# Feed-forward blocks of a decoder trunk: the third block's matmuls on two 64-row tiles of the TensorE array

## Chip, cores, metric

One Trainium2 chip, one core. The metric is the device time of one execution in microseconds (us), as the median of several runs; lower is better. Engines are named as in the profile: PE is TensorE (matmuls), PEld its weight loads, DVE VectorE, ACT ScalarE, POOL GpSimd, SP SyncE, which issues most DMAs.

## What is computed

Two layers of a decoder, 256 tokens, width 1024. Each layer is a feed-forward stage, a token mixer and a second feed-forward stage, each followed by a layer norm:

```python
def _swiglu(x, w1, w3, w2):
    return (jax.nn.silu(x @ w1) * (x @ w3)) @ w2

for l in range(DEPTH):                                   # DEPTH = 2
    h = _swiglu(x, ffn_w1[l, 0], ffn_w3[l, 0], ffn_w2[l, 0])
    x = _layernorm(ALPHA * x + 0.5 * h, ln_g[l, 0], ln_b[l, 0])
    h = _mixer(x, l, ...)                                # gated spatial mixing and differential attention
    x = _layernorm(ALPHA * x + h, ln_g[l, 1], ln_b[l, 1])
    h = _swiglu(x, ffn_w1[l, 1], ffn_w3[l, 1], ffn_w2[l, 1])
    x = _layernorm(ALPHA * x + 0.5 * h, ln_g[l, 2], ln_b[l, 2])
```

x is 256 x 1024; w1 and w3 are 1024 x 2816, w2 is 2816 x 1024, all fp32. There are four feed-forward stages in all.

## The kernel before

**Products.** Each matrix product is made of three fp32r matmuls: an operand is split into a high part (`hi`, ScalarE rounds it to fp32r) and a low part (`lo`, VectorE subtracts), and hi x hi, lo x hi and hi x lo are added up in one bank of the matmul memory (PSUM). `three` (L253) issues them, L256 is the matmul. The contraction runs over the 128 rows of the array. The moving operand is 512 columns wide, one bank.

**Feed-forward stage (`ffn`, L599).** The 2816 inner columns are computed in five blocks of 512 (`for n in range(NB)`, L633) and two further groups (`gemm_a2`, L640), then multiplied by w2 (`gemm_b`). A block is one call of `gemm_b2` (L317); the very first block of the kernel is `gemm_first`. `gemm_b2` takes four banks: two token halves t of 128 tokens, times two matrices m (w1 and w3). The order of TensorE is written by hand: for t, for two halves c of the contraction, for m, for four k-tiles of 128 each: `rows_b` (L287) issues three matmuls per k-tile. So one block has 2 x 2 x 8 x 3 = 96 matmuls of 128 rows by 512 columns. Weights are loaded and split while t = 0 runs (`stream`, L152: a DMA of 1 MB by SyncE, then per 512 columns one ScalarE copy, L178, and one VectorE subtraction, L180) and used again for t = 1. There are eight buffers for each of the high and the low parts, so the next block's weights are split while t = 1 runs, as the buffers come free.

**The way out of a block (`front`, L605).** When a token half is done, `done` (L607) reads the two banks: ScalarE takes SiLU of the first (L612), VectorE multiplies by the second (L613). The result is transposed by POOL copies and a DMA (`transposed`, L204) and split into the operand of w2 (`turned`, L619; L629 and L631). These later steps are started by a counter of matmul work (`beat`).

**Who sets the order.** TensorE's order is that of the program. The other engines' instructions are ordered by a scheduler by priorities; `behind(...)` (L148) adds single constraints, such as that `done` for t = 0 is not placed ahead of the stage's last activation and subtraction of the norm (`latest`).

**Banks.** There are eight: four tagged "main" (`bank`, L78) and four tagged "side" (`side_bank`, L81), each group handed out in turn. In the feed-forward stages the blocks use main banks; side banks serve the mixer's attention and the norms' transposes.

**Two other places that the prediction reads.** The attention scores (`scores`, L698, matmul in L704) have a contraction of 64: plain fp32 matmuls of 64 rows, alternately from the upper and the lower 64 partitions, into two side banks. Each appears in the trace as two matmuls. The last norm (L508) has plain fp32 matmuls on all 128 rows.

Of the kernel before, what the change touches and what calls it, by code (L numbers as in the profile page):

```python
# [16 lines left out]
AF = mybir.ActivationFunctionType  # L17
# [3 lines left out]
P = 128  # L21
D = 1024
T = 256
NT = T // P
# [30 lines left out]
def trunk(ctx, tc, x, xT, w13a, w13b, w2, wb, wqk, wu, wg, wgr, wbr, wbrr, wo, gateb, gatebr, sgug, sgub, sguwT, sgubias, lam, diffg,  # L55
# [22 lines left out]
    def bank():  # L78
        return psum.tile([P, 512], F32, tag="main", name=name("bank"))
# [207 lines left out]
    def rows_b(ps, t, k0, piece, xh, xl, kts, c0=0, n=512, first=0):  # L287
# [6 lines left out]
                  k == first, k == (first - 1) % kts)  # L294
        beat(n / 1024)

    def gemm_b(src, kts, xh, xl, done, tail=4, last=()):

        blocks = [[(bank(), c, n) for c, n in (last if t else ()) or ((0, 512),)] for t in range(NT)]
        held = []  # L300
        for c in range(0, kts, 4):
            nk = min(4, kts - c)
            for i, piece in enumerate(stream(src[:, c * 512 : (c + nk) * 512], nk * 512)):
                k = c + 2 * i
                if k >= kts - tail:
                    held.append((k, piece))
                    continue
                for t in range(NT):
                    for ps, o, n in blocks[t]:
                        rows_b(ps, t, k, piece, xh, xl, kts, o, n)  # L310
        for t in range(NT):
            for ps, o, n in blocks[t]:
                for k, piece in held:
                    rows_b(ps, t, k, piece, xh, xl, kts, o, n)
                done(t, ps[:, :n], o, n)

    def gemm_b2(srcs, xh, xl, done, norm=None, second=(0, 1), each=None):  # L317

        lent, after = [()] * 4, [(None, None)] * 4
        if norm:
            lent = [(0, 1), (0,), (), ()]
            after[1:3] = (None, None if norm.front == 1 else norm.ends[0]), [norm.ends[0]] * 2
        ps = [[bank() for _ in range(2)] for _ in range(NT)]
        got = [[None] * 4 for _ in range(2)]
        for t in range(NT):
            order = second if t else (0, 1)
            for c in order:
                if norm:  # L330
                    norm.ready(t, c)
                    after[3] = [norm.ends[1]] * 2
                for m in range(2):
                    n = 2 * c + m
                    if t == 0:
                        got[m][2 * c : 2 * c + 2] = stream(srcs[m][:, c * CH : (c + 1) * CH], sub=512, lent=lent[n],
                                                           after=after[n], pool=(1,) if norm and norm.front == 1 and n == 1 else ())
                    for i in range(2 * c, 2 * c + 2):
                        rows_b(ps[t][m], t, 2 * i, got[m][i], xh, xl, KT, first=order[0] * KT // 2)
                    if each and c == order[1]:  # L340
                        each(t, m, ps[t][m])
            with behind(latest[0] if t == 0 else None):
                done(t, ps[t])

    def gemm_first(srcs, done):

        step()
        ps = [[bank() for _ in range(2)] for _ in range(NT)]
        raw = [[raw_pool.tile([P, CH], F32, tag="raw", name=name("raw")) for _ in range(2)] for _ in range(2)]
        for k0, nk in ((0, 1), (1, 1), (2, 1), (3, 1), (4, 2), (6, 2)):  # L350
            xr = slots("xraw", 2)[0][:, : nk * T]
            nc.sync.dma_start(xr, xT[:, k0 * T : (k0 + nk) * T])
            c, k = k0 // 4, k0 % 4
            if nk == 2 or k % 2 == 0:
                w = [[p.tile([P, HC], F32R, tag=n, name=name("w" + n)) for p, n in ((hi_pool, "hi"), (lo_pool, "lo"))]
                     for _ in range(2)]
            for m in range(2):
                (A if k0 + m == 0 else nc.sync).dma_start(raw[c][m][:, k * 512 : (k + nk) * 512],
                                                          srcs[m][:, k0 * 512 : (k0 + nk) * 512])
            x = x_cat[c][:, k : k + nk]  # L360
            split(x[:, :, :T], x[:, :, T:], xr.rearrange("p (k t) -> p k t", k=nk))
            ws = [[[v[:, (k + j) % 2 * 512 : (k + j) % 2 * 512 + 512] for v in w[m]] for m in range(2)]
                  for j in range(nk)]
            for j in range(nk):
                for m in range(2):
                    split(*ws[j][m], raw[c][m][:, (k + j) * 512 : (k + j + 1) * 512])
            end = k0 + nk == KT
            for ts in ((0,), (1,)) if end else ((0, 1),):
                for j in range(nk):
                    for m in range(2):  # L370
                        hi, lo = ws[j][m]
                        for y, o in ((hi, 0), (hi, T), (lo, 0)):
                            for t in ts:
                                PE.matmul(ps[t][m], x[:, j, o + t * P : o + (t + 1) * P], y,  # L374
                                          start=k0 + j == 0 and o == 0 and y is hi,
                                          stop=k0 + j == KT - 1 and y is lo)
                        beat(0.25 * len(ts))
                if end:
                    done(ts[0], ps[ts[0]])
# [219 lines left out]
    def ffn(l, f, i, norm, last=False):  # L599
        xh, xl = parts(both)  # L600
        h_hi = [act.tile([P, 512], F32R, tag="slot", name=name("hhi")) for _ in range(FT // 2)]
        h_lo = [act.tile([P, 512], F32R, tag="slot", name=name("hlo")) for _ in range(FT // 2)]
        hh, hl = view(h_hi), view(h_lo)

        def front(n, wait):  # L605

            def done(t, ps):  # L607
                pool, tag = ((act, "val"), (res, "bc"))[n % 2]
                p = pool.tile([P, D], F32, tag=tag, name=name("planes"), bufs=2).rearrange("p (w c) -> p w c", w=2)
                s = p[:, 1]  # L610
                with behind(norm.xhi[1, 0] if norm and (n, t) == (0, 0) else None):
                    silu[0] = A.activation(s, ps[0], AF.Silu).ins  # L612
                added[0] = V.tensor_tensor(out=s, in0=s, in1=ps[1], op=ALU.mult).ins  # L613
                beside(turned(n, t, s, p, wait[t]), 0)
                if norm is None and (n, t) == (1, 0):
                    beside(setup(s[:, :1]), 0)
            return done

        def turned(n, t, s, p, wait):  # L619
            lead = 3.5 if n == 0 and norm else 0  # L620
            yield from transposed(s, p[:, 0], p[:, 1], lead, wait - lead, 0.6, G)
            x = p[:, 0].rearrange("p (k t) -> p k t", k=4)
            yield 0.6
            for j in range(2):
                k = (n * 4 if n < NB - 1 else FT - 4) // 2 + j
                hi, lo = (v[k].rearrange("p (k t) -> p k t", k=2)[:, :, t * P : (t + 1) * P] for v in (h_hi, h_lo))
                f = x[:, 2 * j : 2 * j + 2]
                with behind(silu[0]):
                    A.activation(hi, f, AF.Copy)  # L629
                with behind(added[0]):  # L630
                    V.tensor_tensor(out=lo, in0=f, in1=hi.bitcast(F32), op=ALU.subtract)  # L631

        for n in range(NB):  # L633
            srcs = [w13b[l, f, m * NB + n] for m in range(2)]
            if n == 0 and norm is None:
                gemm_first(srcs, front(n, (10.3, 10.3)))
            else:
                gemm_b2(srcs, xh, xl, front(n, (13.3, 10.3)), norm=norm if n == 0 else None)
        for j in range(FA, FT - 4, 2):
            for m, z in gemm_a2([w13a[l, f, j - FA + m] for m in range(2)], both, lambda m: t512("silu")):  # L640
                s = z[:, :T]
                silu[0] = A.activation(s, s, AF.Silu).ins
                V.tensor_tensor(out=s, in0=s, in1=z[:, T:], op=ALU.mult)
                split(hh(j + m), hl(j + m), s)
        ln = Norm(l, i, 2.0 * ALPHA, 4.0 * EPS, s[:, :1], last)
        gemm_b(w2[l, f, 0], FT, hh, hl, lambda t, p, c, n: ln.part(t, 0, p))

        def done(t, p, c, n):
            ln.part(t, 512 + c, p)
            if c + n == 512:  # L650
                ln.finish(t, 1.9)

        gemm_b(w2[l, f, 1], FT, hh, hl, done, tail=14, last=((0, 256), (256, 256)) if last else ())
        return ln.close()

# [389 lines left out]
```

## Time and profile before

| | |
|---|---|
| median of 3 runs | 1209.79 us (1209.71 to 1209.86) |
| span of the profiled execution | 1208.3 us |
| what lies around the span, by the median | 1.5 us |
| TensorE busy | 1202.6 us, 5891 matmuls |
| VectorE busy | 903.2 us |
| ScalarE busy | 719.9 us |
| POOL busy | 332.9 us |
| fp32r matmuls of L256, 128 x 512, mean of one as recorded | 390 ns |

No time of the profiled execution other than its span is recorded, so the 1.5 us are the difference of the median and the span. A line of the trace names the source line, the engine, the operation, the tile written and the tiles read, the shape (partitions x elements), and the count. "64\*128" in a matmul's line is the part of the array that it uses, rows x columns. A matmul's recorded duration (390 ns) includes its way through the array, and successive matmuls overlap; how fast they follow each other is read from their starts. In the timeline the first number is the start in us from the beginning of the span, the second the time that the merged instructions took, and in brackets stands how long the engine had been idle before and what ended that. "L256" and the like are lines of the kernel before.

### The profile page before, as it was taken

What the parts mean: (1) busy time and instruction counts of PE and PEld (TensorE: products, weight loads), DVE (VectorE), ACT (ScalarE), POOL (GpSimd) and SP (SyncE); (2) the same over time, 40 slices, a digit from 0 to 9 for tenths busy, and PEclk for the clock granted to TensorE, in tenths of its full rate; (3) what the DMA queues carried; (4) which work ended last, traced back from release to release, by engine and by line L of the source; (5) the groups of instructions that cost most, each with busy time, mean ns of one, the idle gap of its engine ahead of it and who ended that gap; (6) DMA issues with size and microseconds to landing.
All of it is one profiled execution on the core that took longest, in us unless ns stands there. A gap on an engine that the chain in (4) does not pass through costs nothing.

```text
span 1208.3 us, 16816 instructions
## 1 busy us (share of the span) xinstructions
PE 1202.6 (100%) x5891; PEld 1013.3 (84%) x5891; DVE 903.2 (75%) x1544; ACT 719.9 (60%) x1388; POOL 332.9 (28%) x442
## 2 busy tenths in 40 slices
PE   9999999999999999999999999999999999999998
PEld 8888888888888888888888888888888888888887
DVE  6686669897689886766686756688966989776763
ACT  6465547668855665554555554576788556564740
POOL 1433101256421234330053330004464012423300
PEclk9999999999999999999999999999999999999999
DMA  9967646768765666767476766476676764877540
GB/s 347 303 219 238 253 174 203 259 200 231 240 213 180 200 231 208 249 201 261 149 245 198 259 187 261 148 273 238 211 205 199 251 192 153 274 231 239 186 181 35
DMA packets 124006, 263.58 MB, mean 218 GB/s; under 512 B 88417, under 2 KB 89489, under 8 KB 97809
## 3 DMA queue, kind: packets, MB, share of 16 engines
q1 hardware_dynamic: 119664, 248.80, 62.0%
q0 software_dynamic: 3824, 13.18, 3.4%
q8 instruction: 46, 0.75, 0.3%
q10 hardware_dynamic: 432, 0.52, 0.1%
q14 instruction: 40, 0.32, 0.1%
HBM read 236.52 MB, written 1.05 MB: 197 GB/s over the span
## 4 chain that ended last, share of the span: by engine, by line
PE 99%; DMA 0%; DVE 0%; ACT 0%; issue 0%; ACTq 0%
PE bank L256 72%; PE bank L268 15%; PE bank L275 8%; PE bank L374 2%; PE sbank L704 1%; PE sbank L760 1%; PE sbank L878 1%; DMA xraw<-in_xT 0%; PE sbank L758 0%; PE sbank L533 0%; PE sbank L512 0%; DVE xtok L520 0%; ACT whi L220 0%; DVE st L471 0%; DVE xtok L467 0%; ACT x L220 0%
## 5 line engine op out<-in xcount | busy, mean ns | idle before, releaser
L180 DVE TENSOR_TENSOR wlo<-raw,whi 128x512 fp32r<-128x512 f32 (+1 forms) x566 | 524.6, 962 | 114.8 <-ACT whi L178 80.0
L178 ACT ACTIVATE whi<-raw 128x512 fp32r<-128x512 f32 (+1 forms) x570 | 433.3, 799 | 246.6 <-PE bank L256 183.0
L256 PE MATMUL bank<-whi,x 128*128 128x512 f32 x1480 | 460.7, 390 | 0.0
L256 PEld LDWEIGHTS bank<-whi,x 128*128 128x128 f32 x1480 | 277.9, 188 | 57.7
L256 PE MATMUL bank<-wlo,x 128*128 128x512 f32 x740 | 288.0, 389 | 0.0
L256 PEld LDWEIGHTS bank<-wlo,x 128*128 128x128 f32 x740 | 139.0, 188 | 28.2
L268 PE MATMUL bank<-x,whi 128*128 128x512 f32 x640 | 153.3, 391 | 0.0
L256 PE MATMUL bank<-whi,hhi 128*128 128x512 f32 (+1 forms) x374 | 141.2, 378 | 0.0
L256 PE MATMUL bank<-wlo,hhi 128*128 128x512 f32 (+1 forms) x374 | 141.0, 377 | 0.0
L256 PE MATMUL bank<-whi,hlo 128*128 128x512 f32 (+1 forms) x374 | 140.9, 377 | 0.0
L193 POOL COPY planes<-planes 128x512 uint16<-128x512 uint16 x80 | 87.1, 1116 | 193.9 <-DVE planes L613 193.9
L268 PEld LDWEIGHTS bank<-x,whi 128*128 128x128 f32 x640 | 118.2, 188 | 23.8
L202 POOL COPY planes<-planes 128x512 uint16<-128x512 uint16 x80 | 70.9, 931 | 95.8 <-DMA planes<-planes 95.5
L613 DVE TENSOR_TENSOR planes<-planes,bank 128x512 f32<-128x512 f32 x40 | 27.4, 684 | 83.8 <-issue 69.3
L612 ACT ACTIVATE planes<-bank 128x512 f32<-128x512 f32 x40 | 23.9, 598 | 102.6 <-PE bank L256 101.5
L275 PEld LDWEIGHTS bank<-x,wlo 128*128 128x128 f32 x640 | 81.4, 191 | 2.9
L275 PE MATMUL bank<-x,wlo 128*128 128x256 f32 x640 | 82.6, 283 | 0.0
L256 PEld LDWEIGHTS bank<-whi,hlo 128*128 128x128 f32 x374 | 70.4, 188 | 13.0
L256 PEld LDWEIGHTS bank<-whi,hhi 128*128 128x128 f32 x374 | 70.4, 188 | 12.8
L256 PEld LDWEIGHTS bank<-wlo,hhi 128*128 128x128 f32 x374 | 70.4, 188 | 12.6
L575 POOL COPY nvia<-ntwo 128x256 uint16<-128x256 uint16 x20 | 10.4, 565 | 198.1 <-DMA ntwo<-nvia 179.9
L680 POOL TENSOR_TENSOR swap<-swap,sin_t 128x512 f32<-128x512 f32 x16 | 27.1, 1695 | 100.0 <-DMA swap<-z 78.0
(209 smaller groups left out, 1392.0 us busy)
## 6 DMA issues: line engine op xcount, KB each, us to landing
raw<-in_w13b SPq DMA_DIRECT2D x76, 1024.0 KB, 5.8
raw<-in_w SPq DMA_DIRECT2D x40, 1024.0 KB, 6.2
raw<-in_wb SPq DMA_DIRECT2D x16, 1024.0 KB, 5.1
raw<-in_wqk SPq DMA_DIRECT2D x16, 1024.0 KB, 6.3
raw<-in_w13a SPq DMA_DIRECT2D x8, 1024.0 KB, 5.1
raw<-in_wgr SPq DMA_DIRECT2D x8, 1024.0 KB, 5.3
raw<-in_wg SPq DMA_DIRECT2D x8, 1024.0 KB, 5.0
raw<-in_wu SPq DMA_DIRECT2D x8, 1024.0 KB, 6.4
```

Source lines behind the costliest of these rows:

```text
L178: A.activation(h, r, AF.Copy)
L180: eng.tensor_tensor(out=w, in0=r, in1=h.bitcast(F32), op=ALU.subtract)
L193: G.tensor_copy(out=planes(out)[:, w], in_=numbers(src)[:, w])
L202: eng.tensor_copy(out=numbers(out)[:, w], in_=planes(src)[:, w])
L256: PE.matmul(ps, xx, w, start=start and n == 0, stop=stop and n == 2)
L268: PE.matmul(b[-1], hi[:, k * P : (k + 1) * P], xc(k), start=k == 0, stop=False)
L275: PE.matmul(b[n][:, :T], lo[:, k * P : (k + 1) * P], xc(k)[:, :T], start=False, stop=k == KT - 1)
L374: PE.matmul(ps[t][m], x[:, j, o + t * P : o + (t + 1) * P], y, start=k0 + j == 0 and o == 0 and y is hi, stop=k0 + j == KT - 1 and y is lo)
L612: silu[0] = A.activation(s, ps[0], AF.Silu).ins
L613: added[0] = V.tensor_tensor(out=s, in0=s, in1=ps[1], op=ALU.mult).ins
L680: turned_by[0] = G.tensor_tensor(out=s3, in0=s3, in1=s, op=ALU.mult).ins
L704: PE.matmul(banks[m][:, j * nk : (j + 1) * nk], rows(qT, m, j, t * P, P), rows(kT, m, j, 0, nk), start=True, stop=True)
```

## The change

In every feed-forward stage, the third block (n = 2) is no longer done by `gemm_b2` but by a new `gemm_two`. Each 128-row matmul becomes two of 64 rows: the upper and the lower half of the contraction, on two 64-row tiles of the array in turn, each adding up in a bank of its own. A token half so needs four banks instead of two: t = 0 takes the four side banks, t = 1 the four main banks. On the way out ScalarE copies the second bank of each pair to SBUF and VectorE adds the first to it; SiLU and the product then read the sums from SBUF. The fourth block (n = 3) takes side banks for its first token half.

```diff
+    def rows_two(banks, t, k0, piece, xh, xl):
+
+        hi, lo = piece
+        for j in range(2):
+            k, s = k0 + j, slice(j * 512, (j + 1) * 512)
+            for n, (y, x) in enumerate(((hi, xh), (lo, xh), (hi, xl))):
+                for half in range(2):
+                    r = slice(half * P // 2, (half + 1) * P // 2)
+                    PE.matmul(banks[half], x(k)[r, t * P : (t + 1) * P], y[r, s], start=k == 0 and n == 0,
+                              stop=k == KT - 1 and n == 2)
+        beat(0.5)
+
+    def gemm_two(srcs, xh, xl, done):
...
+        got = [[None] * 4 for _ in range(2)]
+        for t in range(NT):
+            ps = [[(bank if t else side_bank)() for _ in range(2)] for _ in range(2)]
+            for c in range(2):
+                for m in range(2):
+                    if t == 0:
+                        got[m][2 * c : 2 * c + 2] = stream(srcs[m][:, c * CH : (c + 1) * CH], sub=512)
+                    for i in range(2 * c, 2 * c + 2):
+                        rows_two(ps[m], t, 2 * i, got[m][i], xh, xl)
+            whole = []
+            with behind(latest[0] if t == 0 else None):
+                for a, b in ps:
+                    v = s512("part")
+                    A.activation(v, b, AF.Copy)
+                    V.tensor_tensor(out=v, in0=a, in1=v, op=ALU.add)
+                    whole.append(v)
+            done(t, whole)
...
-    def gemm_b2(srcs, xh, xl, done, norm=None, second=(0, 1), each=None):
+    def gemm_b2(srcs, xh, xl, done, norm=None, second=(0, 1), each=None, first=None):
...
-        ps = [[bank() for _ in range(2)] for _ in range(NT)]
+        ps = [[(t == 0 and first or bank)() for _ in range(2)] for t in range(NT)]
...
+            elif n == 2:
+                gemm_two(srcs, xh, xl, front(n, (13.3, 10.3)))
             else:
-                gemm_b2(srcs, xh, xl, front(n, (13.3, 10.3)), norm=norm if n == 0 else None)
+                gemm_b2(srcs, xh, xl, front(n, (13.3, 10.3)), norm=norm if n == 0 else None,
+                        first=side_bank if n == 3 else None)
```

In the changed kernel the matmul of the half tiles is line 305, the copy out of the second bank L326 and the addition L327; the lines of `done` and later ones are 34 higher than before (L612 is L646).

## The prediction

> **What bounds the kernel now.** I read four views in this order: the page's first lines and its chain, the timeline of ScalarE in a feed-forward stage, the timeline of TensorE at two places, and the busy time of VectorE around the third block.
>
> The page (busy time and share of the span, then the clock in 40 slices, then the chain; a group row gives busy us and mean ns of one, then the idle time before it):
>
> ```profile
> span 1208.3 us, 16816 instructions
> PE 1202.6 (100%) x5891; PEld 1013.3 (84%) x5891; DVE 903.2 (75%) x1544; ACT 719.9 (60%) x1388; POOL 332.9 (28%) x442
> ...
> PEclk9999999999999999999999999999999999999999
> ...
> PE 99%; DMA 0%; DVE 0%; ACT 0%; issue 0%; ACTq 0%
> ```
>
> TensorE is the bound: it is on 99% of the chain, at full clock throughout. The other engines have room. So the change is worth what it does to TensorE's own pace, plus any wait that it creates. The median of the runs, 1209.79 us, is 1.5 us above the profiled span of 1208.3; I sum against the span and add that 1.5 at the end.
>
> ScalarE's SiLU reads the bank that is finished last but one in each token half, so its starts mark equal places of successive halves:
>
> ```profile
> 46.71 0.60 ACT L612 ACTIVATE planes<-bank 128x512 f32<-128x512 f32 x1 [0.21 <-PE bank L256]
> 57.59 0.60 ACT L612 ACTIVATE planes<-bank 128x512 f32<-128x512 f32 x1 [6.55 <-PE bank L256]
> 68.47 0.60 ACT L612 ACTIVATE planes<-bank 128x512 f32<-128x512 f32 x1 [0.21 <-PE bank L256]
> ```
>
> Two halves of 48 matmuls take 68.47 - 46.71 = 21.76 us, 226.7 ns each: no wait between them. What is in those 226.7 ns? The same line with 256 columns (first and last of six rows), and four plain fp32 matmuls on the whole array, 256, 256, 512 and 512 columns wide:
>
> ```profile
> 1200.13 0.28 PE L256 MATMUL bank<-whi,hhi 128*128 128x256 f32 x1
> ...
> 1200.73 0.28 PE L256 MATMUL bank<-whi,hlo 128*128 128x256 f32 x1
> ```
>
> ```profile
> 1200.85 0.38 PE L508 MATMUL sbank<-xtok,ident 128*128 128x256 f32 x1
> 1201.07 0.38 PE L508 MATMUL sbank<-xtok,ident 128*128 128x256 f32 x1
> 1201.28 0.59 PE L508 MATMUL sbank<-xtok,ident 128*128 128x512 f32 x1
> 1201.71 0.59 PE L508 MATMUL sbank<-xtok,ident 128*128 128x512 f32 x1
> ```
>
> 256 columns of fp32r take 0.60/5 = 120 ns, 512 take 226.7. So a column costs 106.7/256 = 0.417 ns, and 120 - 106.7 = **13.3 ns of every fp32r matmul depend on no column**. Plain fp32 pays 0.43/2 = 215 ns for 256 columns and 430 for 512: 0.84 ns a column, and nothing fixed that two decimals show. It loads new weights for each matmul just as fp32r does.
>
> **The change part by part.**
>
> *The matmuls.* A third block has 2 token halves x 2 matrices x 8 k-tiles x 3 products = 96 whole-array matmuls; four feed-forward stages make 384, 87 us of the span. Each becomes two of 64 rows with 512 columns. All hangs on the pitch of such a pair. No fp32r half tile is in this trace, but plain fp32 ones are: the attention scores. Their pairs, by the weight loads that start with them:
>
> ```profile
> 232.42 0.19 PEld L704 LDWEIGHTS sbank<-qk,qk 64*128 64x128 f32 x2
> 232.64 0.19 PEld L704 LDWEIGHTS sbank<-qk,qk 64*128 64x128 f32 x2
> 232.85 0.19 PEld L704 LDWEIGHTS sbank<-qk,qk 64*128 64x128 f32 x2
> 233.07 0.30 PEld L704 LDWEIGHTS sbank<-qk,qk 64*128 64x128 f32 x4
> 233.18 0.31 PEld L704 LDWEIGHTS sbank<-qk,qk 64*128 64x128 f32 x4
> ```
>
> Two loads start within 0.01 us, the next two 0.65/3 = 217 ns later. Here the two halves do run together, and a pair of 256 columns costs what one whole-array fp32 matmul of 256 columns costs (215). The bounds for an fp32r pair of 512 columns follow: 215 ns from below (the fixed part gone, as in these fp32 pairs, which take as long per pair), 2 x 226.7 = 453 from above (no overlap). I take **226.7, a gain of nothing**, by the one equality that the trace does show: a pair costs what the whole matmul of its own type costs. The reason: plain fp32 issues the same load and matmul and has no fixed part, so issuing a matmul with new weights is not what costs 13.3 ns. What differs is that fp32r takes a column every 0.417 ns, half as long. I therefore put the 13.3 ns down to the feed of the rows, and each half tile's rows get as many weights and columns as before.
>
> *Changing between whole and half array.* One visit to the scores, from the last whole matmul before to the second after, and the same two rows of another visit:
>
> ```profile
> 231.78 0.39 PE L268 MATMUL bank<-x,whi 128*128 128x512 f32 x1
> ...
> 232.10 1.58 PE L704 MATMUL sbank<-qk,qk 64*128 64x256 f32 x16
> ...
> 233.61 0.50 PE L268 MATMUL bank<-x,whi 128*128 128x512 f32 x1
> ...
> 233.94 0.39 PE L268 MATMUL bank<-x,whi 128*128 128x512 f32 x1
> ```
>
> ```profile
> 829.23 0.39 PE L268 MATMUL bank<-x,whi 128*128 128x512 f32 x1
> ...
> 831.39 0.39 PE L268 MATMUL bank<-x,whi 128*128 128x512 f32 x1
> ```
>
> Both visits last 2.16 us. At pace they hold two whole matmuls (0.453), four pairs of 256 columns (4 x 0.217) and four of 128 (4 x 0.11): 1.76. So a visit costs **0.40 us**: 0.32 us instead of 0.23 from the last whole matmul to the first pair, 0.33 instead of 0.23 after the return, and the rest in first loads that hide behind nothing. A third block is one visit, both token halves running without a whole matmul between: 4 x 0.40 = **+1.6 us**.
>
> *The way out.* Each of the four bank pairs of a block gets a copy on ScalarE and an addition on VectorE, priced by the nearest rows, SiLU and its product, both from a bank:
>
> ```profile
> L613 DVE TENSOR_TENSOR planes<-planes,bank 128x512 f32<-128x512 f32 x40 | 27.4, 684 | 83.8 <-issue 69.3
> L612 ACT ACTIVATE planes<-bank 128x512 f32<-128x512 f32 x40 | 23.9, 598 | 102.6 <-PE bank L256 101.5
> ```
>
> That is 4 x 0.6 = 2.4 us of ScalarE and 4 x 0.7 = 2.7 us of VectorE per block. What waits behind them is the next block's weights (L178, L180), since the changed order puts them behind the additions:
>
> ```profile
> 60.37 0.69 DVE L613 TENSOR_TENSOR planes<-planes,bank 128x512 f32<-128x512 f32 x1 [5.26 <-issue]
> 60.97 1.74 DVE L631 TENSOR_TENSOR hlo<-planes,hhi 128x256 fp32r<-128x256 f32 x2
> 62.63 8.88 DVE L180 TENSOR_TENSOR wlo<-raw,whi 128x512 fp32r<-128x512 f32 x13
> ...
> 73.39 1.88 DVE L180 TENSOR_TENSOR wlo<-raw,whi 128x512 fp32r<-128x512 f32 x3
> ```
>
> ```profile
> 58.08 0.72 ACT L629 ACTIVATE hhi<-planes 128x256 fp32r<-128x256 f32 x2
> ```
>
> ```profile
> 71.22 0.39 PE L256 MATMUL bank<-wlo,x 128*128 128x512 f32 x1
> ...
> 81.42 0.39 PE L256 MATMUL bank<-wlo,x 128*128 128x512 f32 x1
> ```
>
> TensorE takes the first low part of the fourth block at 71.22; VectorE has thirteen by 71.51, the first 7 us ahead, and the last by 75.27, used at 81.42: 6.1 us ahead. After the first half the changed ScalarE order is copy, SiLU, two splits, second copy. The second copy ends near 57.6 + 0.6 + 0.7 + 0.6 + 0.8 + 0.6 = 60.9, and addition and product follow to 62.3 instead of 61.05: 1.3 us late. The second half adds two more additions, 1.4, and perhaps 0.6 behind a copy. At most 3.3 us late against 6.1 of lead: **cost 0**. TensorE is the cover; without that lead each stage would pay up to 3.3 us. VectorE's 5.26 us of idle time before 60.37 takes the first additions.
>
> *Banks and queues.* The second half uses all four main banks, the first the four side banks, and the fourth block starts on side banks that were read out 10 us earlier: no wait. SyncE issues the same DMAs; at a few places a transpose goes one weight load later, and its result is not wanted before the next matrix product. POOL's order stays. Cost 0.
>
> Sum: 0 + 1.6 + 0 + 0 = +1.6 us; span 1208.3 + 1.6 = 1209.9, time 1209.9 + 1.5 = **1211.4 us**, 0.13% up. About 0.2%, or 2.4 us, is what a measurement of this kernel can tell from no change.
>
> **The rivals.**
>
> *A. The other half covers the fixed part.* If the 13.3 ns are a wait between a matmul and its successor on the same rows that the other tile's stream can fill, pairs run at 215 to 217 ns as the scores do: 384 x (226.7 - 216) = 4.1 us gained, 5.1 if all of the 13.3 goes. Less 1.6: 1209.8 - 2.5 = **1207.3** (1206.3 to 1207.7). For it: the fp32 pairs keep that pace. Against: whole-array fp32 keeps it too, so the half tiles are not what earns it. Chance 0.28, the largest of the rivals, since no fp32r half tile is shown. A rule of the Trainium skill speaks for this rival ("TensorE: Matmul & The Clock Gate", What overlaps and what doesn't, under The mechanism): loads overlap running matmuls only where the row groups differ. By it, part of each load stands bare now and turns would hide it, which makes this rival's 1207.3 the result. The trace contradicts its "only":
>
> ```profile
> 231.56 0.19 PEld L268 LDWEIGHTS bank<-x,whi 128*128 128x128 f32 x1
> ```
>
> This whole-array load starts at 231.56, together with the matmul before it, and is over long before the next at 231.78. So by this row the load is hidden already.
>
> *B. The fixed part is paid twice.* If each 64-row matmul pays its own 13.3 ns in one shared place, a pair costs 240 ns: 384 x 13.3 = 5.1, plus 1.6: **1216.5**, slower. It decides as soon as a pair exceeds 228.8 ns (0.8 us over 384 pairs brings the 2.4). Against: two fp32 halves start within 0.01 us of each other. Chance 0.10. The Trainium skill's span model (same page, Measured speedup vs the span model) gives a packed group one matmul plus about 4 ns for each further tile. If every pair paid that, the estimate would be 1.5 us more, 1212.9; the score pairs, 217 against 215, bear out at most half of it.
>
> *C. fp32r halves do not run together.* Then the change does not do what it says: a pair costs 2 x 213.3 to 2 x 226.7 ns, 384 x 200 to 227 = 77 to 87 us more, about **1292**. For it: the fp32 halves take a column only every 0.84 ns, so two streams at 0.417 are not shown anywhere. Against: 64 rows each are fed no more than now. Chance 0.15.
>
> *D. The way out is late after all.* If a copy waits in a bad place and the lead of 6.1 us is overrun by one to three us in each of four stages, +4 to +12: **1215 to 1223**. Chance 0.05.
>
> **How the numbers follow.** Forecast 0.42, A 0.28, B 0.10, C 0.15, D 0.05. Predicted 1211.4. C can be left out (0.15), and the upper part of D; the range reaches from A's best case to B: 1206.3 to 1217. Faster by over 0.2% (below 1207.4) is some two thirds of A: 0.18. Within 0.2%: the rest of A and most of the forecast, 0.10 + 0.40 = 0.50. Slower: B, C, D and a remainder of the forecast, 0.32.
>
> **What would show it.** In the changed profile, the pitch of line 305's pairs in a third block: 226.7 is the forecast, 216 rival A, 240 B, above 400 C. SiLU's distance across the third block then stays 10.88 us per half but for the visit. Each block should show about 0.3 us between the last whole matmul and the first pair and again after the return, 0.40 in all. TensorE must have no idle time at the start of the fourth block, ended by VectorE or ScalarE; if it has, D is right. The forecast is wrong if the pair's pitch leaves 226.7 by more than 2 ns either way.

## The result and the profile after

The changed kernel takes 1211.82 us (median, 1211.52 to 1212.23) against 1209.83 us before (1209.48 to 1210.40): ratio 1.0016, 95% interval 1.0009 to 1.0022. It is 2.0 us slower; 1211.4 had been forecast.

The page of the changed kernel, the lines that answer to those of before:

```profile
span 1210.1 us, 17622 instructions
PE 1204.4 (100%) x6275; PEld 1012.0 (84%) x6275; DVE 906.1 (75%) x1560; ACT 729.7 (60%) x1404; POOL 335.4 (28%) x442
...
PEclk9999999999999999999999999999999999999999
...
PE 99%; DMA 0%; DVE 0%; ACT 0%; issue 0%; ACTq 0%
```

384 matmuls more (6275 against 5891), and TensorE is busy for 1.8 us more, which is the growth of the span. It is still the whole chain, at full clock. VectorE and ScalarE are busy 3 and 10 us longer, and none of that is seen in the span.

The timeline of TensorE in the first third block, in steady state (start, time of the merged row, then the instructions; each low-part row is one pair, "x2"; rows between are left out):

```profile
54.95 0.39 PE L305 MATMUL sbank<-wlo,x 64*128 64x512 f32 x2
...
58.35 0.39 PE L305 MATMUL sbank<-wlo,x 64*128 64x512 f32 x2
```

Each k-tile has one such row and three pairs, so from 54.95 to 58.35 are fifteen pairs in 3.40 us: **226.7 ns a pair**, the pitch of one whole matmul before. Nothing is gained and nothing lost there. The loss is at the ends of the visit, in the same view, ahead of the block and behind it:

```profile
48.81 0.39 PE L256 MATMUL bank<-whi,x 128*128 128x512 f32 x1
49.12 0.50 PE L305 MATMUL sbank<-whi,x 64*128 64x512 f32 x2
49.46 0.40 PE L305 MATMUL sbank<-wlo,x 64*128 64x512 f32 x2
...
50.16 0.39 PE L305 MATMUL sbank<-wlo,x 64*128 64x512 f32 x2
...
70.81 0.39 PE L305 MATMUL bank<-whi,x 64*128 64x512 f32 x2
71.13 0.50 PE L256 MATMUL sbank<-whi,x 128*128 128x512 f32 x1
71.47 0.40 PE L256 MATMUL sbank<-wlo,x 128*128 128x512 f32 x1
...
72.17 0.39 PE L256 MATMUL sbank<-wlo,x 128*128 128x512 f32 x1
```

Into the half tiles 0.31 us pass where 0.23 would do, then 0.34; back again 0.32 and 0.34. These four steps cost 0.31 + 0.34 + 0.32 + 0.34 - 4 x 0.227 = 0.40 us, as the score visits had it. But the pace has not settled then: the next three pairs take 50.16 - 49.46 = 0.70 us instead of 0.68, the next three whole matmuls 72.17 - 71.47 = 0.70. The weight loads show one thing that is lost at such a change:

```profile
48.58 0.19 PEld L256 LDWEIGHTS bank<-whi,x 128*128 128x128 f32 x1
49.12 0.19 PEld L305 LDWEIGHTS sbank<-whi,x 64*128 64x128 f32 x2 [0.35 <-issue]
```

The load at 48.58 belongs to the matmul at 48.81 and runs 0.23 us ahead of it, beside another matmul. The first loads of the half tiles start together with their own pair, at 49.12, so nothing hides them. SiLU's starts show the whole. This is ScalarE's timeline of the changed kernel (L646 is the former L612, L326 the copy out of the second bank), from the second half of the second block to that of the fourth:

```profile
46.51 0.60 ACT L646 ACTIVATE planes<-bank 128x512 f32<-128x512 f32 x1 [0.21 <-PE bank L256]
57.65 0.60 ACT L326 ACTIVATE part<-sbank 128x512 f32<-128x512 f32 x1 [6.80 <-PE sbank L305]
59.00 0.63 ACT L646 ACTIVATE planes<-part 128x512 f32<-128x512 f32 x1 [0.76 <-DVE part L327]
60.37 0.60 ACT L326 ACTIVATE part<-sbank 128x512 f32<-128x512 f32 x1
...
90.53 0.60 ACT L646 ACTIVATE planes<-bank 128x512 f32<-128x512 f32 x1 [0.20 <-PE bank L256]
```

90.53 - 46.51 = 44.02 us for four halves, where 4 x 10.88 = 43.52 would be the pace of before: 0.50 us for one visit to the half tiles, there and back, and 4 x 0.50 = 2.0 us is the whole result.

### The profile page after: what moved, and what is told of

It is laid out like the page before. It is cut to its first block, busy times and chain, and to the rows that moved or that the text cites. A ratio compares the mean times of both kernels' runs of the same rounds, so it can differ in the third digit from the quotient of the medians.

```text
span 1210.1 us, 17622 instructions
## 1 busy us (share of the span) xinstructions
PE 1204.4 (100%) x6275; PEld 1012.0 (84%) x6275; DVE 906.1 (75%) x1560; ACT 729.7 (60%) x1404; POOL 335.4 (28%) x442
## 4 chain that ended last, share of the span: by engine, by line
PE 99%; DMA 0%; DVE 0%; ACT 0%; issue 0%; ACTq 0%
PE bank L256 61%; PE bank L268 15%; PE bank L275 8%; PE sbank L305 4%; PE sbank L256 4%; PE bank L305 4%; PE bank L408 2%; PE sbank L741 1%; PE sbank L797 1%; PE sbank L915 1%; DMA xraw<-in_xT 0%; PE sbank L795 0%; PE sbank L567 0%; PE sbank L546 0%; DVE xtok L554 0%; ACT whi L220 0%
## 5 line engine op out<-in xcount | busy, mean ns | idle before, releaser
L256 PE MATMUL bank<-whi,x 128*128 128x512 f32 x1096 | 343.1, 390 | 0.0
L256 PEld LDWEIGHTS bank<-whi,x 128*128 128x128 f32 x1096 | 205.8, 188 | 42.7
L256 PE MATMUL bank<-wlo,x 128*128 128x512 f32 x548 | 213.3, 389 | 0.0
L256 PEld LDWEIGHTS bank<-wlo,x 128*128 128x128 f32 x548 | 102.9, 188 | 20.8
L646 ACT ACTIVATE planes<-bank 128x512 f32<-128x512 f32 x28 | 16.8, 599 | 55.6 <-PE bank L256 54.1
L647 DVE TENSOR_TENSOR planes<-planes,bank 128x512 f32<-128x512 f32 x28 | 19.1, 683 | 41.2 <-issue 26.3
```

The costliest lines, as they stand in the source:

```text
L256: PE.matmul(ps, xx, w, start=start and n == 0, stop=stop and n == 2)
```

## The experiments

The theory: a pair of half tiles costs what a whole matmul costs, because the fixed part of 13.3 ns lies in the feed of fp32r columns to the rows, which half tiles do not change; the loss is the change between whole and half array, once per visit; the way out is hidden. Its rivals: the loss lies in the pairs; it lies in the way out; and the fixed part is the price of new weights, not of the type. The kernel before was timed again beside each group of runs, on the same chip, so its median differs a little from run to run (1209.53 to 1210.12). The first expectations put a visit at 0.46 us, less than the 0.50 of SiLU's starts above.

**The way out alone.** All of the change but the half tiles:

```diff
-                for half in range(2):
-                    r = slice(half * P // 2, (half + 1) * P // 2)
-                    PE.matmul(banks[half], x(k)[r, t * P : (t + 1) * P], y[r, s], start=k == 0 and n == 0,
-                              stop=k == KT - 1 and n == 2)
+                PE.matmul(banks[j], x(k)[:, t * P : (t + 1) * P], y[:, s], start=k0 == 0 and n == 0,
+                          stop=k0 == KT - 2 and n == 2)
```

> The changed banks, copies, additions and order, but with whole-array matmuls: even k-tiles add up in one bank and odd ones in the other, no half tile. Theory (way out hidden): 1209.8, no difference from before. Rival 2 (the way out costs what the change lost): 1211.8.

Measured: 1209.66 against 1209.64, ratio 1.0001 (0.9992 to 1.0010). The banks, copies, additions and changed order cost nothing that shows within 0.1%.

**Twice the pairs in as many visits.**

```diff
-            elif n == 2:
+            elif n in (2, 3):
...
-                        first=side_bank if n == 3 else None)
+                        first=side_bank if n == 4 else None)
```

> The fourth block goes on half tiles too, right behind the third: twice the pairs (768), still one visit to the half tiles per stage. Theory (a pair costs a whole matmul, a visit costs 0.46 us as the changed trace has it): the time stays that of the change, 1211.8, ratio to before 1.0016. Rival 1 (the loss is in the pairs, 5 ns each): twice the loss, 1213.8. Rival 2 (the pairs gain and the way out loses more): each doubles, so again about 1213.8; if the pairs gain and only the visits lose, below 1211.8.

Measured: 1211.60 against 1209.64, ratio 1.0016 (1.0007 to 1.0024). The loss is 1.96 us with 768 pairs as it was 1.99 with 384: neither the pairs nor the way out add anything that shows.

**Half the pairs in four times the visits.**

```diff
...
-                        rows_two(ps[m], t, 2 * i, got[m][i], xh, xl)
+                        if m == 0:
+                            rows_two(ps[m], t, 2 * i, got[m][i], xh, xl)
+                        else:
+                            rows_b(ps[m][0], t, 2 * i, got[m][i], xh, xl, KT)
...
```

> In the third block only the first matrix goes on half tiles, the second stays whole: half the pairs (192), but four visits per block instead of one, 16 in all, and half the additions on the way out. Theory: 16 x 0.46 = 7.4 us over before, 1217.2. Rival 1 (the loss is per pair): half of the loss, 1210.8. Rival 2 (the way out loses): half of it, 1210.8.

Measured: 1217.54 against 1209.64, ratio 1.0066 (1.0054 to 1.0079): 7.9 us for 16 visits, 0.49 each. TensorE's timeline of this kernel, a visit's last pair and the whole matmuls up to the next visit:

```profile
52.06 0.39 PE L305 MATMUL sbank<-whi,x 64*128 64x512 f32 x2
52.38 0.50 PE L256 MATMUL sbank<-whi,x 128*128 128x512 f32 x1
52.72 0.40 PE L256 MATMUL sbank<-wlo,x 128*128 128x512 f32 x1
...
55.03 0.39 PE L256 MATMUL sbank<-whi,x 128*128 128x512 f32 x1
55.35 0.50 PE L305 MATMUL sbank<-whi,x 64*128 64x512 f32 x2
```

Each way has the same 0.32 us, and the return has the slow second step too (0.34). With the two runs before, this settles where the time goes: visits times 0.49 us, whatever the number of pairs (4, 4 and 16 visits; 384, 768 and 192 pairs; 2.0, 2.0 and 7.9 us).

**One tile alone.**

```diff
-                for half in range(2):
+                for half in range(1):
                     r = slice(half * P // 2, (half + 1) * P // 2)
...
```

This kernel leaves out half of the third block's contraction, and with it the second banks, the copies and the additions.

> The changed kernel with the upper tile alone: the lower half of the contraction of the third block is left out, with its banks and the additions. Theory (each tile pays the whole 226.7 ns for itself, the second runs beside it for nothing, and the loss is the change between whole and half array): the time of the change, 1211.8, pitch 226.7 on one tile. Rival (two tiles hinder each other, by the few ns between their starts or in their feeds): below 1211.8 by that; and if a 64-row matmul alone has a smaller fixed part, 384 x 13.3 = 5.1 us less at most, 1206.7.

Measured: 1211.68 against 1210.12, ratio 1.0014 (1.0005 to 1.0024). Its timeline, three matmuls of the one tile from row to row:

```profile
52.44 0.39 PE L305 MATMUL sbank<-wlo,x 64*128 64x512 f32 x1
...
55.84 0.39 PE L305 MATMUL sbank<-wlo,x 64*128 64x512 f32 x1
```

Fifteen matmuls take 3.40 us, 226.7 ns each. One tile without its partner is as slow as the pair: 64 rows pay the fixed part as 128 do, and the second tile runs beside the first for nothing.

**Not in turn.**

```diff
-            for n, (y, x) in enumerate(((hi, xh), (lo, xh), (hi, xl))):
-                for half in range(2):
+            for half in range(2):
+                for n, (y, x) in enumerate(((hi, xh), (lo, xh), (hi, xl))):
```

> The changed kernel with the halves not in turn: per k-tile three matmuls on the upper tile, then three on the lower. Theory (matmuls start in program order, and each tile pays 226.7 ns between its own): only the third of one tile and the first of the other overlap, so a k-tile takes four pitches instead of three: 128 x 226.7 ns = 29 us more than the change, 1240.8. Rival (a tile's matmuls start as soon as their own rows are free, whatever stands ahead of them on the other tile): 1211.8.

Measured: 1211.82 against 1210.12, ratio 1.0015 (1.0006 to 1.0024): my expectation was wrong by 29 us, the rival's was right. The timeline of TensorE in this kernel, the visit's first row and three later ones:

```profile
48.90 0.50 PE L305 MATMUL sbank<-whi,x 64*128 64x512 f32 x2
...
54.73 0.40 PE L305 MATMUL sbank<-wlo,x 64*128 64x512 f32 x2
54.95 0.62 PE L305 MATMUL sbank<-whi,x 64*128 64x512 f32 x4
55.41 0.40 PE L305 MATMUL sbank<-wlo,x 64*128 64x512 f32 x2
```

In the program three matmuls of the upper tile stand ahead of the lower tile's three. In the trace the visit's first two matmuls already start as a pair ("x2" at 48.90), and so do the low-part ones at 54.73, which stand three apart. The rows do not name the tile, but two low parts that start together cannot be neighbours in this program. So the lower tile did not wait for those ahead of it on the upper tile. "In turn" is not what makes the halves overlap.

**The type.** In the kernel before, the third block's three products in bf16 on the whole array. The splits write the block's `hi` and `lo` as bf16, and `top` takes the upper 16 bits of an fp32r number:

```diff
...
+            wh, wl = (w[:, j * 512 : (j + 1) * 512] for w in (hi, lo))
+            xx, xy = (top(f(k)[:, t * P : (t + 1) * P]) for f in (xh, xl))
+            three(ps, xx, xy, wh, wl, k == first, k == (first - 1) % kts)
...
```

> The kernel before, with the third block's three products in bf16 on the whole array (the operands of that block lose precision): same count of matmuls, same weight loads of 128 columns, 512 columns each. Theory as the prediction has it (the 13.3 ns belong to feeding 4-byte columns at 0.417 ns each): bf16 has next to no fixed part, about 215 ns a matmul, 384 x 11 = 4.4 us less, 1205.4. Rival 3 (the 13.3 ns come with any change of weights at this pace): 226.7 ns, 1209.8.

Measured: 1206.10 against 1209.64, ratio 0.9970 (0.9959 to 0.9982). TensorE's timeline, low-part rows, three matmuls from one to the next; the first two rows are still fp32r:

```profile
47.61 0.39 PE L258 MATMUL bank<-wlo,x 128*128 128x512 f32 x1
48.29 0.39 PE L258 MATMUL bank<-wlo,x 128*128 128x512 f32 x1
48.98 0.38 PE L258 MATMUL bank<-wlo,x 128*128 128x512 bf16 x1
...
55.45 0.38 PE L258 MATMUL bank<-wlo,x 128*128 128x512 bf16 x1
```

6.47 us for thirty bf16 matmuls, 215.7 ns, each with a weight load of its own: new weights at this pace do not as such cost 13.3 ns. Without its fixed part an fp32r matmul takes 226.67 - 13.33 = 213.3 ns for 512 columns. If a bf16 column takes as long as an fp32r one, the fixed part falls to 215.7 - 213.3 = 2.4 ns. The last run below measures that it does.

**The span of bytes.** The same block in bf16, but the splits write fp32r tiles as in the kernel before, and the matmuls read every second 16-bit word of them in place. Against the run above:

```diff
...
-            wh, wl = (w[:, j * 512 : (j + 1) * 512] for w in (hi, lo))
+            wh, wl = (top(w[:, j * 512 : (j + 1) * 512]) for w in (hi, lo))
...
```

> The kernel before with the third block in bf16 as in the run e4, but read in place from the fp32r tiles, the upper two bytes of every four (that block loses precision): the same bytes are spanned as with fp32r, half of them used. Theory S (the 13.3 ns come with the span of bytes that a column takes in SBUF): 226.7 ns a matmul, 1209.7. Theory E (they come with the type that enters the array): 216 ns, about 1206 as e4.

Measured: 1209.44 against 1209.53, ratio 0.9999 (0.9990 to 1.0008): the gain of bf16 is gone. The same rows of its timeline:

```profile
49.88 0.39 PE L256 MATMUL bank<-wlo,x 128*128 128x512 bf16 x1
...
55.95 0.39 PE L256 MATMUL bank<-wlo,x 128*128 128x512 bf16 x1
```

6.07 us for 27 matmuls, 224.8 ns. The stationary operand, which the weight loads read (here the activations), is read with the same stride in both runs, and its loads are recorded with 98 and 96 ns (188 for fp32r), so the length of the load does not set the pitch. For TensorE only the moving operand differs, in how it lies in SBUF. So most of the fixed part (11.5 of 13.3 ns) comes with a moving operand that spans four bytes per column. Whether a stride in the moving operand would cost as much by itself, for another reason, is not excluded by this run. That half tiles leave the fixed part alone fits: each partition still delivers 512 such columns per matmul.

**Fewer weight columns.**

```diff
...
+            m = P if k in (0, KT - 1) else 96
...
+            xx, xy = (f(k)[:, t * P : t * P + m] for f in (xh, xl))
+            three(ps[:m], xx, xy, wh, wl, k == first, k == (first - 1) % kts)
...
```

> The kernel before, whole array, with weights of 96 instead of 128 columns in six of the eight k-tiles of the third block (the last 32 tokens of each half lose those products). 288 matmuls. Theory W (the 13.3 ns are the weight load's share of a feed that 4-byte columns use up): the fixed part shrinks with the weight columns to 10 ns, 223.3 ns a matmul, 1 us less, 1208.7. Theory M (the 13.3 ns are the start of a 4-byte moving stream): 226.7 ns, 1209.7. The pitch in the trace tells.

Measured: 1210.95 against 1210.12, ratio 1.0009 (1.0000 to 1.0017). Neither number came. Its timeline, three matmuls from row to row:

```profile
651.90 0.39 PE L256 MATMUL bank<-wlo,x 128*96 128x512 f32 x1
...
653.98 0.39 PE L256 MATMUL bank<-wlo,x 128*96 128x512 f32 x1
```

2.08 us for nine, 231 ns: slower than with 128 columns. Theory W falls, since the fixed part did not shrink; theory M does not explain the growth by some 4 ns, whose cause stays open.

**Bf16 for the low parts of the weights alone.** The splits write the low parts of the weights as bf16, and their product takes the upper 16 bits of the activations:

```diff
...
-        for n, (w, xx) in enumerate([(w_hi, xh), (w_lo, xh), (w_hi, xl)]):
+        for n, (w, xx) in enumerate([(w_hi, xh), (w_lo, top(xh)), (w_hi, xl)]):
...
```

> The kernel before, all on the whole array; the low parts of the weights are written in bf16 and multiplied by the upper 16 bits of the high parts of the activations, wherever weights move (blocks, second products, row products), about 1260 matmuls. Theory (the fixed part belongs to fp32r, changing the type costs nothing): 1260 x 10.8 ns = 13.6 us less, 1196. Rival (a change of type between matmuls drains the array as a change to half tiles does, some 0.2 us each): 2500 changes, over 1600.

Measured: 1233.60 against 1210.12, ratio 1.0195 (1.0181 to 1.0209): slower, though far from the rival's number. The timeline:

```profile
652.04 0.39 PE L263 MATMUL bank<-wlo,x 128*128 128x512 bf16 x1
652.08 0.82 PE L263 MATMUL bank<-whi,x 128*128 128x512 f32 x2
652.74 0.39 PE L263 MATMUL bank<-wlo,x 128*128 128x512 bf16 x1
...
654.84 0.39 PE L263 MATMUL bank<-wlo,x 128*128 128x512 bf16 x1
```

Four groups of three take 2.80 us, 700 ns each, where three fp32r matmuls take 680 and 669 had been expected. The change there and back costs about 31 ns, and the gain of one bf16 matmul is 11. The trace has 1302 bf16 weight loads in such groups: 1302 x 20 = 26 us, about the 23.5 us measured. The weight loads show where the time may go:

```profile
652.03 0.10 PEld L263 LDWEIGHTS <-x 128*128 128x128 bf16 x1 [0.27 <-issue]
```

This load starts only 0.01 us ahead of its own matmul at 652.04, where in the changed kernel the load at 48.58 started 0.23 us ahead of its own. So it is not hidden. Whether this is what costs the 31 ns was not tested.

**Bf16 throughout.** Every tile of high and low parts in bf16, the kernel before otherwise:

```diff
...
-                hi = hi_pool.tile([P, HC], F32R, tag="hi", name=name("whi"))
-                lo = lo_pool.tile([P, HC], F32R, tag="lo", name=name("wlo"))
+                hi = hi_pool.tile([P, HC], BF16, tag="hi", name=name("whi"))
+                lo = lo_pool.tile([P, HC], BF16, tag="lo", name=name("wlo"))
...
-                    eng.tensor_tensor(out=w, in0=r, in1=h.bitcast(F32), op=ALU.subtract)
+                    eng.tensor_tensor(out=w, in0=r, in1=h, op=ALU.subtract)
...
```

> The kernel before, every operand split into bf16 high and low parts instead of fp32r ones, on the whole array throughout, so that the type changes only around the plain fp32 matmuls. Each product keeps some 16 bits of its operands instead of more. Theory (the fixed part belongs to fp32r; 10.8 ns each over some 5470 fp32r matmuls of 512 and 256 columns): 59 us less, 1151, if the other engines keep up (VectorE is busy for 903 us in all). Rival (the other engines' splits, hidden by 6 to 8 us until now, come late in some stages): between 1151 and 1200, with idle time of TensorE ended by VectorE or ScalarE.

Measured: **1150.66 against 1209.53**, ratio 0.9516 (0.9500 to 0.9532), 59 us less, as the fixed part had it. Its page and two stretches of its timeline:

```profile
span 1148.6 us, 16693 instructions
PE 1135.6 (99%) x5780; PEld 577.0 (50%) x5891; DVE 895.5 (78%) x1544; ACT 714.9 (62%) x1388; POOL 337.6 (29%) x442
```

```profile
59.82 0.38 PE L255 MATMUL bank<-wlo,x 128*128 128x512 bf16 x1
...
62.41 0.38 PE L255 MATMUL bank<-wlo,x 128*128 128x512 bf16 x1
...
1137.76 0.27 PE L255 MATMUL bank<-whi,hlo 128*128 128x256 bf16 x1
...
1141.04 0.27 PE L255 MATMUL bank<-whi,hlo 128*128 128x256 bf16 x1
```

Twelve matmuls of 512 columns in 2.59 us are 216 ns, and thirty of 256 columns in 3.28 us are 109.3 ns. So a bf16 column takes (215.8 - 109.3)/256 = 0.416 ns, as an fp32r column does to within 0.001, and 109.3 - 106.5 = 2.8 ns depend on no column, near the 2.4 above. TensorE is still busy for 99% of the span: the engines that split and read out keep up. (The trace lacks some matmul records here, 5780 beside 5891 loads, so its busy time is a little low.) This version beats both kernels; it keeps fewer bits of each operand than fp32r parts do.

## Why the prediction was right, step by step

- **A pair costs a whole matmul: right.** 226.7 ns was forecast and 226.7 measured. The forecast itself rested on one likeness, the fp32 pairs of the scores, and had a chance of 0.42; the number alone would not show its reason. The reason given, that the fixed part belongs to the feed of the rows and not to issuing a matmul with new weights, is borne out by two runs: bf16 with new weights each time has 2.4 ns (215.7 in all), and bf16 read with the span of fp32r is back at 224.8. One tile alone, as slow as two, shows that each tile pays it for itself. What in the feed takes the 13.3 ns was not measured, and no run repeats an fp32r matmul without a new weight load, so whether the load has a part in it stays open.
- **A visit costs 0.40 us: the right mechanism, too small.** It was 0.50 (0.49 in the two other runs that count visits). The score visits were read to the second whole matmul after the return; the pace settles only several matmuls later, 0.70 instead of 0.68 us for the next three, on each side. That term is 4 x 0.10 = 0.4 us short, which is the distance of 1211.4 from 1211.8. Why the pace takes so long to settle was not tested.
- **The way out is hidden: right.** The run with the way out alone is equal to before within 0.1%. VectorE's timeline in the changed kernel, and TensorE's last low part of the fourth block's first half, show what the lead became:

```profile
61.72 0.69 DVE L647 TENSOR_TENSOR planes<-planes,part 128x512 f32<-128x512 f32 x1
...
63.42 6.51 DVE L180 TENSOR_TENSOR wlo<-raw,whi 128x512 fp32r<-128x512 f32 x10
...
76.02 0.68 DVE L180 TENSOR_TENSOR wlo<-raw,whi 128x512 fp32r<-128x512 f32 x1
...
81.71 0.39 PE L256 MATMUL sbank<-wlo,x 128*128 128x512 f32 x1
```

  The product ends at 62.41 (62.3 was forecast), and the last low part at 76.70, 1.4 us later than before, where up to 3.3 had been allowed. TensorE uses it at 81.71, 5.0 us after.
- **Rival A** (the other half covers the fixed part) falls by the pitch and by the tile that ran alone: there was nothing that the partner could fill. The load rule of the Trainium skill that spoke for it ("TensorE: Matmul & The Clock Gate", What overlaps and what doesn't) is not borne out: the whole-array load at 231.56 in the prediction ran beside a matmul on the same rows, and turns on two row groups gained nothing.
- **Rival B** falls by the same pitch, and with it the 1212.9 that 4 ns more for every pair would have made. **C** falls by the two halves at one start, **D** by the fourth block's start: from the last pair at 70.81 to 71.13 it is 0.32 us, as at the return in the kernel with four visits, with no wait ended by VectorE or ScalarE.

## What to carry to other kernels

Two half tiles gave a product of full depth nothing here: each tile pays the full time of its columns and the fixed part, and every visit to the half tiles, there and back, costs half a microsecond. So tile only what has no 128 rows to use, and in few visits. Look instead at the pitch of the matmuls against their columns at two widths: what is left over there, 13.3 ns of 226.7 here, is what another form of the operand may save. Here bf16 parts throughout saved 11 ns of it per matmul, 59 us in all, at the price of bits of each operand. If types are mixed, keep matmuls of one type together.

## What the hardware showed unexpectedly

- Matmuls of two row tiles do not wait for each other's place in the program: three of one tile, then three of the other, ran as pairs at 227 ns (54.73 to 55.41 is three).
- A bf16 matmul between fp32r ones costs some 31 ns for the change of type there and back (700 instead of 669 ns per three), more than the 11 ns that it gains.
- After each change between whole and half array the pitch stays some nanoseconds long for several matmuls (0.70 instead of 0.68 us for three).
- Bf16 read in place with a stride of four bytes as the moving operand ran at 224.8 ns, densely stored at 215.7.
- Weights of 96 instead of 128 columns made fp32r matmuls slower, 231 instead of 226.7 ns.
